# Masked keys of a dilated attention kept in residue order, and the products of its sample attention on VectorE

## The chip, the cores and the metric

The kernel runs on one core of a Trainium2 chip. The metric is the device time of one execution in microseconds (us); less is better. Engines: TensorE (PE in the rows; PEld is its weight load), VectorE (DVE), ScalarE (ACT), GpSimd (POOL) and SyncE (SP, which only issues DMAs).

## The reference

One inference step of a two-layer decoder: an attention layer, then a state-space layer, each with a squared-ReLU MLP and layer norms. There are 512 new prompt tokens and 8 sample tokens, one for each of 8 sequences with cached state. The change touches the attention layer. Its 16 heads of 64 run in three groups with dilations 1, 4 and 16:

```python
ATTN_GROUPS = ((128, 1), (512, 4), (2048, 16))
...
    scores = jnp.einsum('brnqhe,brnkhe->brnhqk', qb, kx) * SCALE
...
    scores = jnp.where(mask[None, None, :, None], scores, -jnp.inf)
    mx = jnp.max(scores, -1, keepdims=True)
    p = jnp.exp(scores - mx)
```

A prompt query of group 1 sees only keys whose position differs from its own by a multiple of 4 (group 2: of 16). A sample token attends to cached keys and values (every first, fourth or sixteenth cached position) and its own:

```python
    scores = jnp.einsum('bthe,btshe->bths', q.astype(F32), kg) * SCALE
    ...
    o = jnp.einsum('bths,btshe->bthe', p, vg) / den[..., None]
```

## The kernel before

Activations lie with features on the 128 partitions and tokens along them: 512 prompt tokens and then 8 sample tokens, 520 columns. Dense products split weights and activations into a high and a low part (`whi`, `wlo`) of a reduced fp32 type and add three products of each; they go in two halves of 260 columns (line 246). ScalarE makes the high part of weights and VectorE the low part (lines 185, 189, 196).

The order of all engines' work is written by hand. A *slot* is one dense product of 24 matmuls of 260 columns, followed by its evacuation from PSUM. Between slots, *lanes* (generators that advance by a step twice a slot) and *timers* (`self.after(n, ...)`, due n slots later) add the rest of the work. Every engine executes its own instructions in the order in which they were recorded. The attention layer walks over 8 pairs of heads (`c`) and in each over three groups (`g`): four slots for queries and keys with the rotary embedding (lines 571 to 583 on VectorE), two for values. PSUM has three banks `D` for the slots, three banks `S` for scores, transposes and the like, and two banks `V` for outputs.

What the change touches:

- `heads` (line 596), two slots after the keys: ScalarE writes `Kz`, two copies of the keys `K`, each with one head of the pair masked to zero, in the order of the tokens.
- `attn_scores` (from line 675): queries `F1` are the stationary operand, `Kz` with both heads is the moving one (line 774). Group 0 takes blocks of 128 neighbouring queries and up to 256 neighbouring keys a head. Groups 1 and 2 take residues: for residue j queries j, j+4, ... and the keys likewise, 128 a head; two residues share a bank, so that they make two blocks of scores in each group.
- `prod` (line 735): for the sample tokens, GpSimd multiplies the cached keys `ck` with the queries that a DMA has spread over the partitions (`qb`, issued two slots earlier); one slot later VectorE sums over the features (`total`, line 741).
- `attn_sample` (from line 887, in lane C): after a softmax over 16 rows, VectorE copies the weights into `sp` (lines 914, 915). GpSimd then multiplies three tiles of cached values with them and adds them up (lines 926, 930), 128 or 67 partitions by 1024 columns each; 16 small products on TensorE end the sum (line 936).

Around these, `attn_apply` scales the probabilities (VectorE, line 839, and ScalarE, line 837), transposes them on TensorE into an `S` bank (line 860), evacuates them (`pT`, lines 253 and 255) and multiplies with the values (line 853). `Kt` (lines 714, 716) is VectorE's copy of the transposed keys out of an `S` bank. After the last head pair, the outputs `o` are split into `opart` (lines 233, 234) for the output projection.

Of the kernel before, what the change touches and what calls it, by code (L numbers as in the profile page):

```python
# [11 lines left out]
AF = mybir.ActivationFunctionType  # L12
ALU = mybir.AluOpType
# [4 lines left out]
P = 128  # L18
D = 1024
KD = D // P  # L20
SEQ = 512
# [5 lines left out]
E = 64  # L27
# [52 lines left out]
class Net:  # L80
# [476 lines left out]
    def project_qk(self, g, x, cur, sqk):  # L557

        nc = self.nc
        F1, F2 = self.pair("F")  # L560
        if g != 1:
            cur["K2"] = list(self.pair("K"))
        K = cur["K2"].pop(0)
        cur["F1"][g], cur["F2"][g] = F1, K
        m = {}

        def rope_a(half):
            def f(p1):
                c0 = half * HALF
                m[half] = self.unit("ropem").rearrange("p (i t) -> p i t", i=4)  # L570
                nc.vector.tensor_tensor(out=m[half][:, 0:2], in0=p1.unsqueeze(1).broadcast_to((P, 2, HALF)),  # L571
                                        in1=self.cossin[:, :, c0:c0 + HALF], op=ALU.mult)
            return f

        def rope_b(half):
            def f(p2):
                c0 = half * HALF
                cs = slice(c0, c0 + HALF)
                t = m[half]
                nc.vector.tensor_tensor(out=t[:, 2:4], in0=p2.unsqueeze(1).broadcast_to((P, 2, HALF)),  # L580
                                        in1=self.cossin[:, :, cs], op=ALU.mult)
                nc.vector.tensor_tensor(out=F1[:, cs], in0=t[:, 0], in1=t[:, 3], op=ALU.subtract)
                nc.vector.tensor_tensor(out=F2[:, cs], in0=t[:, 2], in1=t[:, 1], op=ALU.add)
                if half:
                    self.after(1, gather)
                    self.after(2, heads)
            return f

        def gather():
            lo, hi = slice(0, 64), slice(64, P)  # L590
            nc.scalar.activation(out=K[lo], in_=F1[hi], func=AF.Copy)
            nc.scalar.activation(out=K[hi], in_=F2[hi], func=AF.Copy)
            nc.scalar.activation(out=F1[hi], in_=F2[lo], func=AF.Copy)

        def heads():
            kz = self.unit("Kz")[:, 0:2 * SEQ].rearrange("p (h t) -> p h t", h=2)
            for h in range(2):
                nc.scalar.activation(out=kz[:, h], in_=K[:, 0:SEQ], func=AF.Copy, scale=self.hmask[:, h:h + 1])
            cur["Kz"][g] = kz

        for half in range(2):
            self.slot(lambda: self.dense(self.weights(sqk, 0), x, half), rope_a(half))
            self.slot(lambda: self.dense(self.weights(sqk, 1), x, half), rope_b(half))
# [74 lines left out]
    def attn_scores(self, c, g, cur, o, late):  # L678

        nc = self.nc  # L680
        F1, F2 = cur["F1"][g], cur["F2"][g]
        kb = self.blocks(F2, g)
        out = self.O[2 + g][0, 0].rearrange("t k (c h) e -> t k c (h e)", h=2)[:, :, c, :]
# [40 lines left out]
        nk = self.NK[g]  # L724
# [9 lines left out]

        def prod():
            q = cur["qb"]
            nc.gpsimd.tensor_tensor(out=q[0:nk], in0=q[0:nk], in1=cur["ck"][g][0:nk], op=ALU.mult)  # L737
            cur["qp", g] = q

        def total():  # L740
# [2 lines left out]
        self.after(1, store)  # L743
        self.after(3, spread)
        self.after(5, prod)
        self.after(6, total)
        if g == 2:
# [7 lines left out]
        kz = cur["Kz"][g]  # L755
        both = lambda t: t.rearrange("p (h k) -> p h k", h=2)
        pts = []
        for js in ((0,), (1,), (2,), (3,)) if g == 0 else ((0, 1), (2, 3)):
            if not pts:
                pts = list(self.pair("prob"))  # L760
            pt = pts.pop(0)
            b = self.bank("S", "s", NSB)
            tiles, q0 = [], 0
            for j in js:
                if g == 0:
                    n = P if j == 0 else 2 * P
                    k0 = max(j - 1, 0) * P
                    q, ks = F1[:, j * P:(j + 1) * P], slice(k0, k0 + n)
                    mask = self.m0[:, 2 * P - n:2 * P]
                else:  # L770
                    n = P
                    q, ks = F1[:, j:SEQ:4], slice(j, SEQ, 4)
                    mask = self.m0[:, P:2 * P] if g == 1 else self.m2
                nc.tensor.matmul(both(b[:, q0:q0 + 2 * n]), q, kz[:, :, ks], start=True, stop=True)  # L774
                for h in range(2):
                    cs = slice(q0, q0 + n)
                    tiles.append((b[:, cs], pt[:, cs], mask, st[:, 1 if g else 0, j, h, g], neg[:, h, j:j + 1]))
                    for i in range(n // P):
                        key = j if g else j - (n // P - 1) + i
                        cur["P"][g, h, j, key] = pt[:, q0 + i * P:q0 + (i + 1) * P]  # L780
                    q0 += n
            a, j1 = 1 if g else 0, js[-1] + 1
            mx, ng = st[:, a, js[0]:j1, :, g, 0], neg[:, :, js[0]:j1].rearrange("p h j -> p j h")
            yield
            for sc, pr, mask, one, _ in tiles:
                nc.vector.tensor_tensor_reduce(out=pr, in0=sc, in1=mask, scale=1.0, scalar=NEG,  # L786
                                               op0=ALU.add, op1=ALU.max, accum_out=one[:, 0:1])
            nc.vector.tensor_scalar(out=ng, in0=mx, scalar1=-SCALE, scalar2=None, op0=ALU.mult)  # L788
            self.after(1, lambda tiles=tiles: self.exps(tiles))
            yield  # L790
# [96 lines left out]
    def attn_sample(self, c, cur, o):  # L887
        nc = self.nc
        nk = self.NK
# [23 lines left out]
        sp = self.sp.tile([P, 3, 16], F32, name="sp", tag="sp")  # L913
# [4 lines left out]
        v0 = cur["cv"][0]  # L918
# [4 lines left out]
        for i in range(3):  # L923
            n = nk[i]
            v = cur["cv"][i][0:n].rearrange("p b (h e) -> p (b h) e", h=2)
            nc.gpsimd.tensor_tensor(out=v, in0=v, in1=sp[0:n, i, :].unsqueeze(2).broadcast_to((n, 16, E)), op=ALU.mult)
            yield
            yield
            if i:
                nc.gpsimd.tensor_tensor(out=v0[0:n], in0=v0[0:n], in1=cur["cv"][i][0:n], op=ALU.add)  # L930
                yield
                yield
        yield
# [685 lines left out]
```

## Time and profile before

| | |
|---|---|
| median of three runs | 2050.95 us (2046.38 to 2053.96) |
| profiled execution, its own time | 2047.91 us |
| its span, first to last instruction | 2045.7 us |
| TensorE busy | 1946.1 us |
| VectorE busy | 1306.1 us |
| ScalarE busy | 938.4 us |
| GpSimd busy | 395.8 us |
| mean granted TensorE clock | 0.975 of full |

The attention layer's head pairs take the first 620 us or so of the span, its end runs to about 740 us, and the rest belongs to the MLPs and the state-space layer. Busy times are sums over instructions; the ends of matmuls are modelled, so that a row's duration is longer than the spacing of starts. How fast TensorE goes is read from the starts of successive rows in its timeline.

### The profile page before, as it was taken

How to read it: one execution, taken by the hardware profiler on the slowest of the kernel's cores; microseconds unless marked ns; L12 is line 12 of the kernel's file. 1: busy time of each engine (PE TensorE's matmuls, PEld its weight loads, DVE VectorE, ACT ScalarE, POOL GpSimd, SP SyncE). 2: the span in 40 equal slices, each digit the busy share in tenths (PEclk: the TensorE clock that was granted, in tenths of full speed). 3: DMA queues.
4: the chain of work that ended last, by engine and by line, in shares of the span. 5: the costliest groups of instructions: out<-in, count | busy, mean ns of one | idle time of the engine just before them, and what ended most of it. 6: DMA issues, size and time to landing. Idle time of an engine off the chain costs nothing. (4 is left out here: it accounts for less than half of the span.)

```text
span 2045.7 us, 38476 instructions
## 1 busy us (share of the span) xinstructions
PE 1946.1 (95%) x15530; PEld 1863.7 (91%) x15530; DVE 1306.1 (64%) x2597; ACT 938.4 (46%) x2071; POOL 395.8 (19%) x230
## 2 busy tenths in 40 slices
PE   7999999999999899999999998988999898999997
PEld 7989898898897789999999998988999898999997
DVE  4575675766868774333335779998887875554335
ACT  4555454554545354435253554644454363425241
POOL 0030330312305330000003023322232331110002
PEclk9999999999998999999999998999999999999998
DMA  7565554455557528454653255545565759996311
GB/s 196 164 174 139 159 141 138 137 159 166 164 166 215 152 68 278 165 194 146 206 196 124 94 170 176 191 154 162 183 205 184 254 154 278 286 283 182 95 42 43
DMA packets 423194, 346.92 MB, mean 170 GB/s; under 512 B 33036, under 2 KB 408292, under 8 KB 421344
## 3 DMA queue, kind: packets, MB, share of 16 engines
q1 hardware_dynamic: 405608, 344.26, 54.4%
q10 hardware_dynamic: 17408, 0.20, 0.5%
q8 instruction: 122, 2.00, 0.4%
q14 instruction: 56, 0.46, 0.1%
HBM read 322.41 MB, written 130.99 MB: 222 GB/s over the span
## 5 line engine op out<-in xcount | busy, mean ns | idle before, releaser
L246 PE MATMUL psd<-x,whi 128*128 128x260 f32 x5920 | 1117.8, 290 | 13.1 <-DVE zz L1169 5.0
L246 PEld LDWEIGHTS psd<-x,whi 128*128 128x128 f32 x5920 | 927.2, 191 | 40.1 <-issue 23.2
L246 PE MATMUL psd<-x,wlo 128*128 128x260 f32 x2960 | 842.8, 285 | 0.5 <-DVE wlo L196 0.5
L246 PEld LDWEIGHTS psd<-x,wlo 128*128 128x128 f32 x2960 | 563.9, 191 | 0.8 <-DVE wlo L196 0.8
L196 DVE TENSOR_TENSOR wlo<-wraw,whi 128x1024 fp32r<-128x1024 f32 (+1 forms) x321 | 395.1, 1250 | 52.0 <-ACT whi L189 40.0
L246 PE MATMUL psd<-hid,whi 128*128 128x260 f32 (+2 forms) x2048 | 372.9, 284 | 7.2 <-DVE acc L484 7.2
L189 ACT ACTIVATE whi<-wraw 128x1024 fp32r<-128x1024 f32 x225 | 234.4, 1050 | 223.8 <-PE psd L246 156.4
L246 PEld LDWEIGHTS psd<-hid,whi 128*128 128x128 f32 x2048 | 318.6, 190 | 7.5 <-DVE acc L484 7.4
L246 PE MATMUL psd<-hid,wlo 128*128 128x260 f32 (+2 forms) x1024 | 290.7, 284 | 0.0
L246 PEld LDWEIGHTS psd<-hid,wlo 128*128 128x128 f32 x1024 | 194.3, 190 | 0.0
L486 DVE TENSOR_TENSOR acc<-acc,psd 128x260 f32<-128x260 f32 (+2 forms) x176 | 74.0, 423 | 168.1 <-PE psd L246 167.9
L537 DVE TENSOR_TENSOR hid<-relu,hid 128x260 fp32r<-128x260 f32 x128 | 60.7, 475 | 165.0 <-ACT hid L534 164.9
L737 POOL TENSOR_TENSOR qb<-qb,cache 128x1024 f32<-128x1024 f32 (+1 forms) x24 | 59.3, 2470 | 474.1 <-DMA qb<-newscr 351.6
L530 ACT ACTIVATE relu<-psd 128x260 f32<-128x260 f32 x128 | 49.6, 387 | 169.5 <-PE psd L246 166.5
L246 PE MATMUL psd<-ypart,whi 128*128 128x260 f32 x512 | 103.0, 299 | 13.9 <-DVE ypart L1438 4.8
L796 ACT ACTIVATE prob<-prob,neg 128x128 f32<-128x128 f32 (+1 forms) x192 | 79.7, 418 | 57.6 <-DVE neg L788 51.7
L246 PEld LDWEIGHTS psd<-ypart,whi 128*128 128x128 f32 x512 | 83.0, 198 | 16.4 <-DVE ypart L1438 5.7
L774 PE MATMUL s<-Kz,F 128*128 128x256 f32 (+1 forms) x192 | 96.1, 617 | 0.0
L571 DVE TENSOR_TENSOR ropem<-psd,trig 128x520 f32<-128x520 f32 x48 | 33.5, 698 | 92.9 <-PE psd L246 87.8
L1079 DVE SCALAR_TENSOR_TENSOR conv<-raw,cvcols,conv 128x511 f32<-128x511 f32 (+2 forms) x96 | 83.1, 865 | 7.4 <-ACT conv L1074 5.1
L489 POOL TENSOR_TENSOR ln_tot<-acc 128x260 f32<-128x260 f32 x6 | 7.1, 1188 | 361.1 <-DVE acc L486 339.1
L786 DVE CUSTOM_DVE_ANT_0 prob<-s,cb 128x128 f32<-128x128 f32 (+1 forms) x192 | 51.5, 317 | 39.8 <-PE s L774 39.2
(253 smaller groups left out, 2546.1 us busy)
## 6 DMA issues: line engine op xcount, KB each, us to landing
wraw<-in_mlp_w_dram SPq DMA_DIRECT2D x128, 512.0 KB
wraw<-in_attn_w_in_dram SPq DMA_DIRECT2D x72, 512.0 KB
wraw<-in_ssm_w_in_dram SPq DMA_DIRECT2D x49, 512.0 KB
cache<-in_cache_kv_w_dram SPq DMA_DIRECT2D x32, 512.0 KB
state<-in_state_ssm_dram SPq DMA_DIRECT2D x32, 512.0 KB
out_dram<-in_cache_kv_w_dram SPq DMA_DIRECT2D x16, 1016.0 KB
qb<-newscr SPq DMA_DIRECT2D x16, 512.0 KB
ab<-acs SPq DMA_DIRECT2D x16, 512.0 KB
```

The lines of the kernel that those rows point to most:

```text
L189: nc.scalar.activation(out=hi, in_=s.raw[0], func=AF.Copy)
L196: self.nc.vector.tensor_tensor(out=lo, in0=src, in1=hi.bitcast(F32), op=ALU.subtract)
L246: self.nc.tensor.matmul(out, a, b[:, cs], start=n == 0, stop=n == 3 * len(w) - 1)
L486: nc.vector.tensor_tensor(out=a, in0=a, in1=ps, op=ALU.add)
L530: nc.scalar.activation(out=t[:, 0], in_=ps, func=AF.Relu)
L537: nc.vector.tensor_tensor(out=h[m][1][:, cs], in0=t[:, 1], in1=h[m][0][:, cs].bitcast(F32), op=ALU.subtract)
L571: nc.vector.tensor_tensor(out=m[half][:, 0:2], in0=p1.unsqueeze(1).broadcast_to((P, 2, HALF)), in1=self.cossin[:, :, c0:c0 + HALF], op=ALU ...
L737: nc.gpsimd.tensor_tensor(out=q[0:nk], in0=q[0:nk], in1=cur["ck"][g][0:nk], op=ALU.mult)
L774: nc.tensor.matmul(both(b[:, q0:q0 + 2 * n]), q, kz[:, :, ks], start=True, stop=True)
L786: nc.vector.tensor_tensor_reduce(out=pr, in0=sc, in1=mask, scale=1.0, scalar=NEG, op0=ALU.add, op1=ALU.max, accum_out=one[:, 0:1])
L796: self.nc.scalar.activation(out=pr, in_=pr, func=AF.Exp, scale=SCALE, bias=ng, accum_out=st[:, 1:2])
L1079: nc.vector.scalar_tensor_tensor(out=t[:, j:SEQ], in0=raw[:, 0:SEQ - j], scalar=w[:, 3 - j:4 - j], in1=t[:, j:SEQ], op0=ALU.mult, op1=ALU.add)
```

## The change

`Kz` of groups 1 and 2 is written in the order of residues: all keys at positions 0, 4, 8, ..., then 1, 5, 9, ..., and so on. ScalarE reads `K` in steps of 4 columns and writes neighbouring ones; the score products of these groups then read 128 neighbouring columns of each head. The queries, still the stationary operand, are taken in steps of 4 as before. Besides, the products `prod` and the products and sums over the cached values are issued on VectorE and no longer on GpSimd: 24 + 24 + 16 instructions.

```diff
@@ heads, line 596
+            src = K[:, 0:SEQ] if g == 0 else K[:, 0:SEQ].rearrange("p (m r) -> p r m", r=4)
             for h in range(2):
-                nc.scalar.activation(out=kz[:, h], in_=K[:, 0:SEQ], func=AF.Copy, scale=self.hmask[:, h:h + 1])
+                dst = kz[:, h] if g == 0 else kz[:, h].rearrange("p (r m) -> p r m", r=4)
+                nc.scalar.activation(out=dst, in_=src, func=AF.Copy, scale=self.hmask[:, h:h + 1])
@@ prod, line 737
-            nc.gpsimd.tensor_tensor(out=q[0:nk], in0=q[0:nk], in1=cur["ck"][g][0:nk], op=ALU.mult)
+            nc.vector.tensor_tensor(out=q[0:nk], in0=q[0:nk], in1=cur["ck"][g][0:nk], op=ALU.mult)
@@ attn_scores, line 772
-                    q, ks = F1[:, j:SEQ:4], slice(j, SEQ, 4)
+                    q, ks = F1[:, j:SEQ:4], slice(j * P, (j + 1) * P)
@@ attn_sample, lines 926 and 930
-            nc.gpsimd.tensor_tensor(out=v, in0=v, in1=sp[0:n, i, :].unsqueeze(2).broadcast_to((n, 16, E)), op=ALU.mult)
+            nc.vector.tensor_tensor(out=v, in0=v, in1=sp[0:n, i, :].unsqueeze(2).broadcast_to((n, 16, E)), op=ALU.mult)
...
-                nc.gpsimd.tensor_tensor(out=v0[0:n], in0=v0[0:n], in1=cur["cv"][i][0:n], op=ALU.add)
+                nc.vector.tensor_tensor(out=v0[0:n], in0=v0[0:n], in1=cur["cv"][i][0:n], op=ALU.add)
```

Lines after 598 stand two lines further down in the changed kernel. On TensorE, ScalarE and SyncE the same instructions stand in the same order as before.

On VectorE, here is the stretch in the second head pair in which the weights `sp` of the first pair's sample tokens come out, before the change (`wlo` is the split of projection weights, `ropem` and `F` the rotary embedding, `ss` the sum of the sample scores):

```order
L571 TENSOR_TENSOR ropem<-psd,trig 128x520
L914 COPY sp<-sP 128x32
L915 COPY sp<-sP 67x16
L255 COPY pT<-pT 128x512
L196 TENSOR_TENSOR wlo<-wraw,whi 128x8x64 x4
L580 TENSOR_TENSOR ropem<-psd,trig 128x520
L582 TENSOR_TENSOR F<-ropem 128x260
L583 TENSOR_TENSOR F<-ropem 128x260
L741 TENSOR_REDUCE ss<-qb 128x16
L839 TENSOR_SCALAR prob<-prob,fac 128x128 x4
L571 TENSOR_TENSOR ropem<-psd,trig 128x520
L716 COPY Kt<-kT 128x512
```

The same stretch on VectorE after the change:

```order
L571 TENSOR_TENSOR ropem<-psd,trig 128x520
L739 TENSOR_TENSOR qb<-qb,cache 128x1024
L916 COPY sp<-sP 128x32
...
L583 TENSOR_TENSOR F<-ropem 128x260
L743 TENSOR_REDUCE ss<-qb 128x16
L928 TENSOR_TENSOR cache<-cache,sp 128x1024
L841 TENSOR_SCALAR prob<-prob,fac 128x128 x4
L571 TENSOR_TENSOR ropem<-psd,trig 128x520
L928 TENSOR_TENSOR cache<-cache,sp 128x1024
L718 COPY Kt<-kT 128x512
```

A query product (line 739) now stands after the first rope product, and two of the value products (line 928) ahead of the copy `Kt`; the remaining three instructions of this chain follow behind it, one slot apart.

GpSimd's queue before the change, from its first product to the second head pair's:

```order
L737 TENSOR_TENSOR qb<-qb,cache 128x1024 x2
L737 TENSOR_TENSOR qb<-qb,cache 67x1024
L737 TENSOR_TENSOR qb<-qb,cache 128x1024
L926 TENSOR_TENSOR cache<-cache,sp 128x1024 x2
L930 TENSOR_TENSOR cache<-cache 128x1024
```

After it, GpSimd's first work is that of the layer's end:

```order
L426 TENSOR_TENSOR acc<-x 128x520 x8
L489 TENSOR_TENSOR ln_tot<-acc 128x260
L491 TENSOR_TENSOR ln_tot<-ln_tot,acc 128x260 x6
```

All its instructions between the head pairs' start and there are gone.

## Rows read from the trace of the kernel before

**Rows 1.** The page, part 1: engine, busy us (share of span), instructions.

```profile
PE 1946.1 (95%) x15530; PEld 1863.7 (91%) x15530; DVE 1306.1 (64%) x2597; ACT 938.4 (46%) x2071; POOL 395.8 (19%) x230
```

**Rows 2.** Waits of TensorE, 0 to 620 us: us in total, times, longest.

```profile
PE pT L860 <- DVE Kt L716: 9.6, 5, 2.0
```

**Rows 3.** Timeline of TensorE, group 0: start us, us, engine, line, operation, tiles, count.

```profile
56.23 0.28 PE L246 MATMUL psd<-x,wlo 128*128 128x260 f32 x1
56.35 1.02 PE L774 MATMUL s<-Kz,F 128*128 128x512 f32 x2
56.81 0.80 PE L246 MATMUL psd<-x,whi 128*128 128x260 f32 x2
57.44 0.28 PE L246 MATMUL psd<-x,wlo 128*128 128x260 f32 x1
```

**Rows 4.** Timeline of TensorE, a block of scores of group 2.

```profile
98.21 2.08 PE L774 MATMUL s<-Kz,F 128*128 128x256 f32 x4
99.70 0.82 PE L246 MATMUL psd<-x,whi 128*128 128x260 f32 x2
100.36 0.28 PE L246 MATMUL psd<-x,wlo 128*128 128x260 f32 x1
```

**Rows 5.** Timeline of GpSimd, 131 to 145 us.

```profile
131.91 4.22 POOL L926 TENSOR_TENSOR cache<-cache,sp 128x1024 f32<-128x1024 f32 x2 [2.57 <-issue]
...
141.33 2.74 POOL L930 TENSOR_TENSOR cache<-cache 67x1024 f32<-67x1024 f32 x1
```

**Rows 6.** Timeline of VectorE, 130 to 148 us; in brackets the idle time before.

```profile
130.98 0.70 DVE L571 TENSOR_TENSOR ropem<-psd,trig 128x520 f32<-128x520 f32 x1 [1.04 <-PE psd L246]
...
132.45 9.35 DVE L196 TENSOR_TENSOR wlo<-wraw,whi 128x512 fp32r<-128x512 f32 x4
...
142.44 1.92 DVE L582 TENSOR_TENSOR F<-ropem 128x260 f32<-128x260 f32 x1
144.29 0.42 DVE L583 TENSOR_TENSOR F<-ropem 128x260 f32<-128x260 f32 x1
...
147.14 0.68 DVE L716 COPY Kt<-kT 128x512 f32<-128x512 f32 x1
```

**Rows 7.** Timeline of TensorE, the first of the five waits.

```profile
147.87 0.55 PE L860 MATMUL pT<-cb,prob 128*128 128x128 f32 x3 [1.98 <-DVE Kt L716]
```

**Rows 8.** Line 774 by itself: weight loads, ns least/median/most, first and last start.

```profile
L774 PEld LDWEIGHTS s<-Kz,F x192: 187/310/333, 49.2 to 655.7; 128*128 128x128 f32 x192
```

**Rows 9.** Timeline of TensorE, transposes of keys in steps of 4.

```profile
70.13 0.65 PE L694 MATMUL kT<-cb,K 128*128 128x128 f32 x4
70.61 0.27 PE L700 MATMUL nT<-cb,F 128*8 128x128 f32 x1
```

**Rows 10.** Line 1467, another layer's sum of two SBUF tiles on VectorE.

```profile
L1467 DVE TENSOR_TENSOR state<-state,Bb x8: 1217/1219/1222, 1672.8 to 1859.4; 128x1024 f32<-128x1024 f32 x8
```

**Rows 11.** Windows: length, busy us of each engine, granted clock (PEclk), DMA share, GB/s.

```profile
226.00:233.00 7.00, 5.17 (x32) 4.68 (x33) 5.40 (x22) 3.59 (x9) 0.00 (x0) 0.76 0.70 206
...
640.00:660.00 20.00, 17.47 (x97) 14.00 (x98) 13.53 (x33) 8.12 (x23) 7.37 (x3) 0.74 0.81 249
```

**Rows 12.** Timelines of VectorE and TensorE, 638 to 644 us.

```profile
638.87 4.23 DVE L234 TENSOR_TENSOR opart<-o,opart 128x520 fp32r<-128x520 f32 x2 [0.26 <-ACT opart L233]
...
640.38 0.39 PE L246 MATMUL psd<-opart,whi 128*128 128x260 f32 x1 [1.10 <-DVE opart L234]
...
643.15 0.58 PE L246 MATMUL psd<-opart,whi 128*128 128x260 f32 x1 [2.15 <-DVE opart L234]
```

**Rows 13.** Timelines of ScalarE and TensorE, masked keys and their scores, group 2.

```profile
79.15 1.32 ACT L598 ACTIVATE Kz<-K,cb 128x512 f32<-128x512 f32 x2
...
93.39 2.08 PE L774 MATMUL s<-Kz,F 128*128 128x256 f32 x4
```

**Rows 14.** Timelines of GpSimd and VectorE, a query product and VectorE's place for it.

```profile
207.71 2.40 POOL L737 TENSOR_TENSOR qb<-qb,cache 128x1024 f32<-128x1024 f32 x1 [26.94 <-PE s L774]
...
211.01 0.70 DVE L571 TENSOR_TENSOR ropem<-psd,trig 128x520 f32<-128x520 f32 x1 [0.29 <-PE psd L246]
```

## The prediction

> **What bounds the kernel now.** I read the busy times first: TensorE is busy 1946 of 2046 us, VectorE 64% [rows 1]. So time is won where TensorE itself works slowly or where it waits. The waits of TensorE in the first 620 us (the attention layer) come second: one kind stands out, five waits of about 1.9 us, 9.6 us together, of a transpose of the probabilities for VectorE's copy of the transposed keys [rows 2]. Everything else there runs without a gap, so a microsecond taken out of TensorE's own instructions in this stage is a microsecond of the span.
>
> Third, the timeline of TensorE around two kinds of score products. Products of fp32 operands show as two records each. In the first group two records read 512 neighbouring columns each; from their start to the start of the weight product behind the next pair 56.35 to 57.44, 1.09 us pass [rows 3]. In the other groups four records read 256 columns each, every fourth of `Kz`: the same 1024 columns, with the same pair behind them, take 98.21 to 100.36, 2.15 us [rows 4]. Ordinary weight products start 0.12 us apart [rows 3], so the pair is 0.24 us of both; 256 neighbouring columns cost (1.09 - 0.24) / 4 = 0.21 us, 256 strided ones (2.15 - 0.24) / 4 = 0.48 us.
>
> Fourth, what makes VectorE late at the five waits: GpSimd's chain of products and sums over the cached values runs from 131.91 to 144.07 [rows 5]; in that stretch VectorE's four weight splits take 9.35 us and a subtraction of 260 columns 1.92 us, while the like one right after GpSimd has ended takes 0.42 [rows 6]. VectorE's instructions with two operands in SBUF thus stand still while GpSimd has one of its own. `Kt` is copied at 147.14, and TensorE, waiting since 145.89, goes on at 147.87 [rows 6, 7].
>
> **The sum.** It is made against the profiled execution, 2047.91 us with a span of 2045.7; the median of the three runs is 2050.95, 3 us above it, inside their own spread of 7.6.
>
> (a) *Scores from neighbouring columns.* Groups 1 and 2 have two blocks of four records in each of 8 head pairs: 32 blocks, each 2.15 - 1.09 = 1.06 us dearer than neighbouring columns, 33.9 us in all. The stationary operand `F1[:, j:SEQ:4]` stays strided: its load takes 310 ns at the median against 187 at the least [rows 8]. The first load of a block has only a 0.12 us product to hide under, so I charge it the difference, 0.12 us. The later three lie under 0.21 us products. If all of a 310 ns load had to pass, each would add 0.10, 0.42 a block in all. But the transposes of the keys also load strided fp32 weights and start (70.61 - 70.13) / 4 = 0.12 us apart, as ordinary products do [rows 9], so a load's latency is longer than the time that it holds the array up. I take 1.06 - 0.12 = 0.94 us a block: **30.1 us**, with ends 20.5 (0.64 a block) and 33.9.
>
> (b) *The five waits.* One instruction of 128x1024 with two SBUF operands costs VectorE 1219 ns when undisturbed [rows 10], 0.61 us per 512 columns. In the chain above VectorE lost 9.35 - 4 x 0.61 = 6.9 and 1.92 - 0.42 = 1.5, 8.4 us. In the new order three moved instructions stand ahead of that `Kt` copy, 3 x 1.22 = 3.7 us. So `Kt` is ready some 4.7 us sooner, at about 143.1 instead of 147.8. TensorE asks at 145.9, or 1 us sooner by (a): 1.8 us to spare, and the waits go: **9.6 us**.
>
> (c) *The clock after them.* [...]
>
> (d) *The end of the layer.* At 640 and 643 TensorE waits 1.10 and 2.15 us for the splits of `opart`, whose two instructions take 4.23 us [rows 12], as long as the splits of (b) did beside GpSimd; at 0.70 each, as the rope product of 520 columns takes [rows 6], they save 2.8. The 20 us from 640 on have a granted clock of 0.74 [rows 11], a loss of 5.2; I count half, 2.5, since later idle stretches there stay: **5.3 us**, ends 0 and 8.
>
> (e) *What VectorE takes over.* 24 products of queries and keys, 24 of values and weights, 16 sums: 64 x 1.22 = 78 us. Before, GpSimd's 64 cost VectorE about as much by blocking it (8.4 us for the five of one head pair, against 6.1), so its load hardly rises, and at 64% it isn't the bound. If none is exposed this costs 0, if every one delays TensorE 78 us. The nearest row is the chain in (b), which has room, so I charge **2 us**.
>
> (f) *At no cost.* ScalarE now reads `K` in steps of four when it writes `Kz`. A pair of these takes 1.32 us [rows 13]. No row shows such a read on ScalarE; bounds are 1.32 and, at TensorE's own ratio 0.48 / 0.21, 3.0 us. The tightest place of groups 1 and 2 has the pair done at 79.15 + 1.32 = 80.47 and the scores at 93.39, 12.9 us of cover [rows 13]; what queues behind it on ScalarE (exponentials, copies of `V`) is later by 1.7 us at worst, twice in a head pair, on an engine that is busy 46% [rows 1]. No DMA changes its place on SyncE's queue. A product now waits in VectorE's queue for the query rows that a DMA spreads: GpSimd started one at 207.71, so they had landed, and VectorE comes to its place after the rope product of 211.01 ends at 211.71, 4 us later [rows 14]. That is the least cover that I found in the even stretch, and the block taken out of it by (a) leaves 3 us.
>
> Sum: 30.1 + 9.6 + 5.0 + 5.3 - 2 = 48; 2047.9 - 48 = **2000 us**.
>
> **The rivals.**
>
> *The loads pace the scores.* If a strided load can't lie under the product before it, the records go on following at about 0.48 us though their columns are neighbours: (a) falls to nothing, and the change would not do what it says for the scores. 2048 - 20 + 2 = 2030 us. Against it: key transposes at 0.12 us with loads of that kind [rows 9], and neighbouring 512-column records whose loads cost nothing visible [rows 3]. Chance 5%. [...]
>
> *The products take GpSimd's place.* VectorE works strictly in order, and two products stand right before the `Kt` copy. If the probabilities' transposes still find their bank occupied, (b) to (d) are lost: 2048 - 30 = 2018 us at the most. The 1.8 us to spare speak against it. Chance 10%; half of it lost would be 2008.
>
> *Slower: VectorE held by the spread of the queries.* All 24 query products now stand in VectorE's queue before weight splits and rope products. Should the spread land later than VectorE arrives, TensorE runs out of split weights. From 3 us beyond today's landing on, each microsecond costs 24; the gain of 48 is used up at 2 us more, 5 us late; 7 us late would be 2000 + 24 x 4 = 2096 us. Speaking for it: before, only GpSimd waited there, with nothing urgent behind. Against: 4 us of cover [rows 14]; and the landing follows TensorE's slots as VectorE's place does, so both come earlier together. Chance 2%.
>
> **How the numbers follow.** Forecast 83%, rivals 5, 10 and 2%. The bounds of (a) and (d) alone give 2000 + 10 + 5 = 2015 and 2000 - 4 - 3 - 2 = 1991. With the second rival and the 3 us between profile and median, the range is 1988 to 2018. About 0.5%, 10 us, is what a measurement of this kernel can tell from no change. Only loads that pace the scores together with half-kept waits come within it (2%); slower is the third rival (2%); faster 96%.
>
> **What would show it.** In the profile after: score records of groups 1 and 2 some 0.21 to 0.24 us apart, a block with its pair near 1.2 us; the row of TensorE waiting for `Kt` gone from the waits; weight splits in the attention layer at 0.7 us throughout; GpSimd idle there; the 64 products on VectorE near 1.22 us. I am wrong in (a) if the block stays above 1.5 us, in (b) and (e) if TensorE's waits for VectorE in the first 620 us sum to over 5 us, in (f) if VectorE waits for the spread or TensorE for `Kz`.

## The result, and the profile after

| | before | after |
|---|---|---|
| median of four runs | 2049.73 us | 1999.84 us (1998.01 to 2001.34) |
| ratio, 95% interval | | 0.9763 (0.9743 to 0.9783) |
| profiled execution: its own time, span | 2047.91, 2045.7 us | 1999.22, 1997.2 us |
| mean granted TensorE clock | 0.975 | 0.978 |

The kernel became 2.4% faster, some 49 us, and the forecast of 2000 us held. Part 1 of the page of the changed kernel (engine, busy us, share, instructions), beside [rows 1]:

```profile
PE 1909.8 (96%) x15530; PEld 1851.4 (93%) x15530; DVE 1287.1 (64%) x2661; ACT 953.7 (48%) x2071; POOL 244.9 (12%) x166
```

VectorE has 64 instructions more, 78 us of work, and is busy 19 us less. Its other instructions thus take about 97 us less than beside GpSimd's products, an estimate from these two busy times. ScalarE has the same instructions and is busy 15 us longer.

The waits of TensorE, 0 to 620 us, in the changed kernel (us in total, times, longest), beside [rows 2]:

```profile
PE xT L312 <- DMA xtok<-in_x_prompt_dram: 5.0, 1, 5.0
PE vT L662 <- ACT Vt L667: 3.4, 1, 3.4
...
PE sT L897 <- DVE ss L743: 1.4, 1, 1.4
...
PE pT L862 <- ACT Vt L667: 0.7, 1, 0.7
```

The row of `Kt` is gone. What is left lies in the first 40 us of the program (`xT` and three smaller rows, as before), in one place of 0.7 us as before, and in the end of the layer, which now begins at 596 us and so falls into this stretch (`vT`, `sT`, a wait of 1.1 us for `opart`).

TensorE's timeline at a block of scores of group 2 in the changed kernel (start us, us, engine, line, tiles), beside [rows 4]:

```profile
94.74 1.19 PE L776 MATMUL s<-Kz,F 128*128 128x256 f32 x4
95.58 0.59 PE L246 MATMUL psd<-x,whi 128*128 128x260 f32 x2
96.01 0.28 PE L246 MATMUL psd<-x,wlo 128*128 128x260 f32 x1
```

From 94.74 to 96.01 the block with its pair takes 1.27 us; the same block took 2.15. Over all 32 blocks the median is 1.27 (1.24 to 1.38), and before 2.15 (2.10 to 2.36), leaving out the five that held a `Kt` wait as well; unrounded, 2.152 - 1.266 = 0.89 us less.

VectorE's timeline in the changed kernel, the stretch of [rows 6] one head pair's chain long (in brackets the idle time before):

```profile
126.56 0.70 DVE L571 TENSOR_TENSOR ropem<-psd,trig 128x520 f32<-128x520 f32 x1 [1.74 <-PE psd L246]
127.17 1.22 DVE L739 TENSOR_TENSOR qb<-qb,cache 128x1024 f32<-128x1024 f32 x1
...
129.09 2.48 DVE L196 TENSOR_TENSOR wlo<-wraw,whi 128x512 fp32r<-128x512 f32 x4
...
132.21 0.43 DVE L582 TENSOR_TENSOR F<-ropem 128x260 f32<-128x260 f32 x1
...
134.03 1.22 DVE L928 TENSOR_TENSOR cache<-cache,sp 128x1024 f32<-128x1024 f32 x1
...
136.56 1.22 DVE L928 TENSOR_TENSOR cache<-cache,sp 128x1024 f32<-128x1024 f32 x1
137.69 0.69 DVE L718 COPY Kt<-kT 128x512 f32<-128x512 f32 x1
```

The four splits take 2.48 us where they took 9.35, and the subtraction of 260 columns 0.43 where it took 1.92. From the first rope product to `Kt` 11.13 us pass; before it was 147.14 - 130.98 = 16.16 [rows 6]. `Kt` is copied by 138.38, and TensorE comes to the transposes of the probabilities behind it 2.0 us later, without a wait:

```profile
140.42 0.60 PE L862 MATMUL pT<-cb,prob 128*128 128x128 f32 x4
```

VectorE runs undisturbed like this up to 577 us. In the last head pair GpSimd's sums of the layer's end (line 426, 577.66 to 597.41) stand beside VectorE, and there one split takes 1.94 us where the like ones take 1.21, and one product of cached values 2.33 where the others take 1.22.

The clock over the even part of the layer, one window each (us, busy us of PE, PEld, DVE, ACT, POOL, granted clock, DMA share, GB/s), first of the kernel before, then of the changed one:

```profile
40.00:600.00 560.00, 549.73 (x4159) 497.70 (x4158) 378.10 (x926) 286.91 (x777) 121.86 (x51) 0.99 0.54 152
```

```profile
40.00:600.00 560.00, 558.20 (x4463) 522.44 (x4462) 400.83 (x1062) 329.27 (x851) 14.28 (x8) 1.00 0.59 169
```

The end of the layer did not become even. TensorE's timeline there in the changed kernel, from the first product of the output projection, beside the last two of [rows 12]:

```profile
596.52 0.39 PE L246 MATMUL psd<-opart,whi 128*128 128x260 f32 x1
598.02 0.39 PE L246 MATMUL psd<-opart,whi 128*128 128x260 f32 x1 [1.11 <-DVE opart L234]
...
615.55 0.23 PE L897 MATMUL sT<-cb,ss 67*16 67x67 f32 x1 [1.41 <-DVE ss L743]
619.15 1.13 PE L662 MATMUL vT<-cb,V 128*128 128x128 f32 x4 [3.37 <-ACT Vt L667]
...
626.65 0.99 PE L862 MATMUL pT<-cb,prob 128*128 128x128 f32 x4 [3.56 <-ACT Vt L667]
...
672.56 0.60 PE L359 MATMUL ln<-ln_tot,ones_d 128*128 128x260 f32 x2
```

The same two points in the kernel before:

```profile
638.89 0.39 PE L246 MATMUL psd<-opart,whi 128*128 128x260 f32 x1
...
719.79 0.60 PE L359 MATMUL ln<-ln_tot,ones_d 128*128 128x260 f32 x2
```

They divide the gain. The first product of the output projection starts at 596.52 instead of 638.89: 42.4 us. The first sum of the layer norm behind it starts at 672.56 instead of 719.79: 47.2. The span is 48.5 shorter. The 1.3 us behind the norm I don't explain. That part has the same instructions in all kernels here, and from the first product with the MLP's `hid` to the last transposition of the outputs it took between 1235 and 1243 us in the profiled executions, 1235 and 1241 in the two of the changed kernel.

### The profile page after: what moved, and what is told of

It reads as the page before. It is cut to its first block, busy times and chain, and to the rows that moved or that the text cites. A ratio compares the mean times of both kernels' runs of the same rounds, so it can differ in the third digit from the quotient of the medians.

```text
span 1997.2 us, 38379 instructions
## 1 busy us (share of the span) xinstructions
PE 1909.8 (96%) x15530; PEld 1851.4 (93%) x15530; DVE 1287.1 (64%) x2661; ACT 953.7 (48%) x2071; POOL 244.9 (12%) x166
## 5 line engine op out<-in xcount | busy, mean ns | idle before, releaser
L196 DVE TENSOR_TENSOR wlo<-wraw,whi 128x1024 fp32r<-128x1024 f32 (+1 forms) x321 | 348.7, 1105 | 54.4 <-ACT whi L189 42.2
L426 POOL TENSOR_TENSOR acc<-x 128x520 f32<-128x520 f32 x8 | 14.3, 1805 | 582.7 <-PE nT L702 577.2
L246 PE MATMUL psd<-ypart,wlo 128*128 128x260 f32 x256 | 74.9, 293 | 0.0
L776 PE MATMUL s<-Kz,F 128*128 128x256 f32 (+1 forms) x192 | 67.9, 462 | 0.0
L1157 ACT ACTIVATE raw<-psd 128x260 f32<-128x260 f32 x64 | 24.4, 382 | 89.9 <-PE psd L246 89.7
```

What stands on the lines that cost most here:

```text
L196: self.nc.vector.tensor_tensor(out=lo, in0=src, in1=hi.bitcast(F32), op=ALU.subtract)
L246: self.nc.tensor.matmul(out, a, b[:, cs], start=n == 0, stop=n == 3 * len(w) - 1)
L426: nc.gpsimd.tensor_tensor(out=acc[m], in0=x[m][0].bitcast(F32), in1=x[m][1].bitcast(F32), op=ALU.add)
L1157: nc.scalar.activation(out=raws[i][:, cs], in_=ps, func=AF.Copy)
```

## The experiments

### One half of the change at a time

The keys alone: three lines go back to GpSimd.

```diff
-            nc.vector.tensor_tensor(out=q[0:nk], in0=q[0:nk], in1=cur["ck"][g][0:nk], op=ALU.mult)
+            nc.gpsimd.tensor_tensor(out=q[0:nk], in0=q[0:nk], in1=cur["ck"][g][0:nk], op=ALU.mult)
...
-                nc.vector.tensor_tensor(out=v0[0:n], in0=v0[0:n], in1=cur["cv"][i][0:n], op=ALU.add)
+                nc.gpsimd.tensor_tensor(out=v0[0:n], in0=v0[0:n], in1=cur["cv"][i][0:n], op=ALU.add)
```

> Only the keys in residue order; all 64 products stay on GpSimd. Theory: the two parts of the change are separate terms. In the changed kernel a block of scores with its pair of products takes 1.27 us at the median instead of 2.16, 32 x 0.89 = 28.5 us. The five waits for Kt stay, and since Kt does not move while TensorE comes 0.9 us sooner, each gets 0.9 us longer: 28.5 - 4.5 = 24 us less, 2026 us, five waits of about 2.8 us, and ScalarE's masked keys at 1.2 us as in the changed kernel. Rival (the keys do nearly all of it): 2000 to 2010 us, waits gone.

The products alone: lines 597 to 600 and 774 as before the change, the products on VectorE.

> Only the 64 products moved to VectorE; the scores read every fourth column as before. Theory: the five waits (9.6 us), three half-clock windows (5 us) and about 4 us at the end of the layer go: 18 us less, 2032 us; score blocks stay at 2.16 us. Rival (keys do nearly all): 2045 us or more. Rival (products take GpSimd's place): the waits for Kt stay, 2045 to 2055 us.

Measured: the keys alone 2033.2 us, ratio 0.9922 (0.9908 to 0.9937), some 16 us; the products alone 2025.16 us, 0.9884 (0.9869 to 0.9899), some 24 us. Both ratios gain 40 us together, the whole change 49, so some 9 us belong to neither half. The traces show it more sharply: TensorE starts the output projection 12.0 us sooner with the keys alone (626.85), 15.9 sooner with the products alone (623.03) and 42.4 sooner with both, so that 14.5 us there need both halves. The keys alone fell short of their expectation, and the products alone, expected at 2032 us, did better than theirs. The wait for `Kt` with the keys alone, TensorE, 0 to 620 us:

```profile
PE pT L862 <- DVE Kt L718: 14.0, 5, 2.9
```

And the 10 us around the first of the five, as a window (granted clock third from the end), of the same kernel; the other four read 0.83 as well:

```profile
140.00:150.00 10.00, 7.20 (x44) 6.67 (x44) 6.65 (x27) 5.56 (x11) 1.53 (x1) 0.83 0.39 105
```

The keys' gain of 32 x 0.89 = 28.5 us is there, block by block. But TensorE comes to the five places sooner, while `Kt` still comes when GpSimd lets VectorE go: the waits are 14.0 us instead of 9.6. The clock falls after all five, where before it fell after three (0.83 in such windows there, 1.00 after the first and the fifth): 2 x 0.17 x 10 = 3.4 us more. So 7.8 us of the 28.5 are handed back there. Just ahead of the output projection this kernel's timeline of TensorE has two further waits:

```profile
622.71 0.48 PE L862 MATMUL pT<-cb,prob 128*128 128x128 f32 x1 [4.15 <-DVE prob L841]
625.01 0.69 PE L862 MATMUL pT<-cb,prob 128*128 128x128 f32 x2 [1.82 <-DVE prob L841]
```

Both are for the scaling of probabilities on VectorE, four instructions that take 10.53 us while GpSimd runs its products and sums without a pause; in the kernel before, the median of one is 0.28 us. VectorE's timeline:

```profile
614.62 10.53 DVE L841 TENSOR_SCALAR prob<-prob,fac 128x128 f32<-128x128 f32 x4
```

The granted clock from 615 us to the output projection is 0.79, another 2.5 us. Up to there 30 of the 32 blocks lie, and 26.7 - 7.8 - 6.0 - 2.5 = 10.4 us, against the 12.0 measured: the shortfall is accounted for to within 2 us. With the products alone the mean clock of 40 to 620 us is 1.00, and the row of `Kt` is gone.

### Which products matter

The 40 instructions over the cached values on VectorE, all else as before the change:

> Of the products only the 40 over the cached values go to VectorE; the 24 query products stay on GpSimd, scores as before. Theory: the value chain of 12 us without a pause is what holds VectorE up ahead of Kt, so nearly all of the gain of the moved products is here: waits for Kt gone, 14 to 17 us less, 2033 to 2036 us. Rival (it is the number of GpSimd's instructions that counts, 40 of 64): about 11 us less, 2038.

The 24 query products on VectorE, all else as before the change:

> Of the products only the 24 query products go to VectorE; the value chain stays on GpSimd, scores as before. Theory: the five waits for Kt stay, a little longer by the product that now stands ahead of them; 0 to 3 us less, 2047 to 2050 us. Rival (number of instructions, 24 of 64): 7 us less, 2043.

Measured: the values alone 2027.53 us, 0.9896 (0.9878 to 0.9914), faster than I expected and close to all products together; the row of `Kt` is gone there too. The queries alone 2056.55 us, 1.0042 (1.0031 to 1.0053): slower by some 9 us, where I expected a small gain. TensorE's wait in that kernel, 0 to 620 us:

```profile
PE pT L860 <- DVE Kt L716: 15.4, 5, 3.1
```

VectorE's timeline there, the chain of [rows 6]:

```profile
131.09 0.70 DVE L571 TENSOR_TENSOR ropem<-psd,trig 128x520 f32<-128x520 f32 x1 [1.74 <-PE psd L246]
131.71 1.22 DVE L737 TENSOR_TENSOR qb<-qb,cache 128x1024 f32<-128x1024 f32 x1
...
133.62 9.41 DVE L196 TENSOR_TENSOR wlo<-wraw,whi 128x512 fp32r<-128x512 f32 x4
...
148.35 0.67 DVE L716 COPY Kt<-kT 128x512 f32<-128x512 f32 x1
```

The query product stands ahead of `sp`, which starts GpSimd's chain. The whole chain, with the time that VectorE loses to it, moves back by 1.2 us: from the rope product to `Kt` 17.26 us instead of 16.16. Nothing is taken off GpSimd in that stretch to pay for it. The waits grew by 5.8 us, and in the 10 us around them the clock's loss sums to 10.9 instead of 5.1; the output projection starts 12.6 us later. So one product of 1.22 us ahead of a chain that stays on GpSimd costs more than its own length, and the same product beside the moved chain costs nothing that the times show (2025.16 us with the query products moved too, 2027.53 without).

### What the stationary operand in steps of four costs

A probe: the score products take 128 neighbouring columns of the queries, so that each block holds the scores of other queries.

```diff
-                    q, ks = F1[:, j:SEQ:4], slice(j * P, (j + 1) * P)
+                    q, ks = F1[:, j * P:(j + 1) * P], slice(j * P, (j + 1) * P)
```

> The changed kernel, but groups 1 and 2 take 128 neighbouring queries as the stationary operand where every fourth is due: other queries' scores, the same work. Theory: the rest of the block's cost over neighbouring columns (1.27 against 1.09 us with its pair) is the strided load of the queries: loads fall from 320 to 190 ns, blocks to 1.09 to 1.12 us, 32 x 0.16 = 5 us less than the changed kernel's 2000, 1995 us. Rival (the four-record block has a cost of its own, or two heads' columns do): blocks stay near 1.27 us, 2000 us.

Measured in a single run: 1993.75 us. A single time does not tell 5 us (a single run of the kernel with strided writes, below, took 1995.57 us, and its output projection starts when that of the changed kernel does), so the trace has to: the output projection starts at 592.3 us instead of 596.5. The weight loads of this line (ns least/median/most), first of the changed kernel, then of the probe:

```profile
L776 PEld LDWEIGHTS s<-Kz,F x192: 187/320/332, 48.4 to 606.5; 128*128 128x128 f32 x192
```

```profile
L776 PEld LDWEIGHTS s<-Kz,F x192: 186/189/193, 48.9 to 602.5; 128*128 128x128 f32 x192
```

A block with its pair takes 1.10 us at the median (1.08 to 1.20), as neighbouring columns in group 0 do [rows 3]. The strided load thus costs 1.266 - 1.101 = 0.16 us a block and 5.3 us in all. The load itself is 0.13 us longer.

### The moved products: room and landing

The query products one slot sooner, nearer to the landing of their spread:

```diff
-        self.after(5, prod)
-        self.after(6, total)
+        self.after(4, prod)
+        self.after(5, total)
```

> The changed kernel with the query products and the sums over them one slot sooner, one slot after the spread was issued and no longer two. It tests the rival in which VectorE waits for the spread's landing. Theory: the cover was 3 us, a slot is 2.9 us: VectorE waits 0 to 1 us for some of the 24, in sum under 12 us, TensorE rides over it on its banks: 2000 to 2004 us. Rival (landing is on VectorE's path): 2 us or more each, 24 x 2 = 48 us, 2040 us and more.

Measured 2000.56 us, 0.9752 (0.9724 to 0.978), like the changed kernel. Idle time of VectorE ahead of line 739 (us, times), first in the changed kernel, then one slot sooner:

```profile
  DMA qb<-newscr: 0.3, 1
```

```profile
  DMA qb<-newscr: 5.9, 4
```

With a slot less of cover the landing does show, in 4 of 24 places. Three of them (1.66, 1.05 and 1.09 us, before 200 us) leave no wait on TensorE. The fourth, at the layer's end, does: VectorE's and then TensorE's timeline,

```profile
617.11 1.22 DVE L739 TENSOR_TENSOR qb<-qb,cache 67x1024 f32<-67x1024 f32 x1 [2.15 <-DMA qb<-newscr]
```

```profile
618.73 0.58 PE L246 MATMUL psd<-opart,whi 128*128 128x260 f32 x1 [2.72 <-DVE acc L484]
```

The sum `acc` stands right behind that product in VectorE's queue. So VectorE's slack swallows the landing in the even stretch and not at the layer's end.

Each query product and each sum of the values with a second instruction beside it whose result nothing reads: 40 instructions, 49 us.

```diff
+            ck = cur["ck"][g][0:nk]
+            nc.vector.tensor_tensor(out=ck, in0=ck, in1=ck, op=ALU.mult)
...
+                nc.vector.tensor_tensor(out=cur["cv"][i][0:n], in0=cur["cv"][i][0:n], in1=cur["cv"][i][0:n], op=ALU.mult)
```

> The changed kernel with 40 more VectorE instructions of the same kind (1.22 us each, on tiles that are dead then): one behind each query product and one behind each sum of the values, 49 us of VectorE work. It tests whether VectorE's added work lies off TensorE's path. Theory: there is room; of 49 us less than 8 come through, 2000 to 2008 us, no wait of TensorE for Kt over 0.5 us before 590 us. Rival (VectorE's room is used up): 25 to 49 us more, 2025 to 2049, with waits for Kt back.

Measured 2008.82 us, 0.9793 (0.9769 to 0.9818): 6 us (by the ratios) to 9 us (by the medians) of the 49 come through, about the 8 that I had set as the limit. TensorE's waits of that kernel that differ from the changed kernel's, 0 to 620 us:

```profile
PE pT L864 <- ACT Vt L667: 4.1, 6, 0.7
...
PE kT L696 <- DVE sp L919: 1.2, 1, 1.2
```

No wait for `Kt` has come back. What is late first is ScalarE's `Vt`, by 0.7 us at six places, one in a head pair (one place in the changed kernel), and then the layer's end. The single load of moved work is therefore near the edge of the room, not beyond it. For `Kt` the test is a mild one: of the 40 only one stands ahead of it in the stretch of [rows 6], where it is copied 139.46 - 127.07 = 12.39 us after the rope product instead of 11.13, and TensorE comes 1.7 us after it instead of 2.0.

### Where the stride should stand

ScalarE reads neighbouring keys and writes them 128 columns apart:

```diff
-            src = K[:, 0:SEQ] if g == 0 else K[:, 0:SEQ].rearrange("p (m r) -> p r m", r=4)
+            src = K[:, 0:SEQ] if g == 0 else K[:, 0:SEQ].rearrange("p (m r) -> p m r", r=4)
...
-                dst = kz[:, h] if g == 0 else kz[:, h].rearrange("p (r m) -> p r m", r=4)
+                dst = kz[:, h] if g == 0 else kz[:, h].rearrange("p (r m) -> p m r", r=4)
```

> The changed kernel with ScalarE reading neighbouring keys and writing them 128 columns apart (same result, the stride on the other side). The changed kernel's masked keys took up to 1.295 us against 0.71 before. Theory: it is the reading in steps of 16 bytes that costs, writing apart costs nothing: 0.71 us each, ScalarE 15 us less busy, the span unchanged (2000 us within 0.3%), since the pair has over 10 us of cover. Rival (any step costs ScalarE): 1.2 us or more each, span unchanged as well.

VectorE puts queries and keys of groups 1 and 2 into residue order as it makes them, so that ScalarE, the key transposes and both operands of the scores read neighbours:

```diff
+            out = F[:, 0:SEQ].rearrange("p (r m) -> p m r", r=4)[:, m0:m0 + n // 4]
+            nc.vector.tensor_tensor(out=out, in0=v(a), in1=v(b), op=op)
...
-                    q, ks = F1[:, j:SEQ:4], slice(j * P, (j + 1) * P)
+                    q, ks = F1[:, j * P:(j + 1) * P], slice(j * P, (j + 1) * P)
```

> A version built on the changed kernel: VectorE writes queries and keys of groups 1 and 2 in the order of residues right at the rotary embedding, so that the masking, the transposes of the keys and both operands of the scores use neighbouring columns. Theory: score blocks with their pair fall from 1.27 to 1.09 us (5 us in all), the transposes of keys lose 0.01 us each (0.8 us), ScalarE's masked keys return to 0.71 us: 5 to 6 us less than the changed kernel, 1994 us, if VectorE's writes 128 columns apart cost nothing (0.43 us for 260 columns). Rival: such writes cost VectorE 1.5 times or more; then still 1994 to 2000, with VectorE busier by 64 x 0.2 = 13 us.

The changed kernel again, timed beside it:

> The changed kernel itself, on the same chip as the version before it. Theory: 2000 us, ratio to the kernel before 0.976.

Measured: 1995.57 us in a single run for the first, 1991.27 us, 0.9726 (0.9704 to 0.9748), for the second, and 1997.28 us, 0.9752 (0.9731 to 0.9773), for the changed kernel on the same chip. Durations of the instructions that make `Kz` (ns least/median/most): in the changed kernel 707/1207/1295, with strided writes

```profile
L600 ACT ACTIVATE Kz<-K,cb x48: 708/1198/1257, 38.2 to 578.5; 128x512 f32<-128x512 f32 x48
```

and with VectorE's residue order, where the strided writes are VectorE's (428/430/433 for 260 columns in the changed kernel)

```profile
L612 ACT ACTIVATE Kz<-K,cb x48: 707/713/722, 37.9 to 572.8; 128x512 f32<-128x512 f32 x48
L583 DVE TENSOR_TENSOR F<-ropem x64: 599/628/656, 45.9 to 567.4; 128x260 f32<-128x260 f32 x32, 128x252 f32<-128x252 f32 x32
```

On ScalarE reading every fourth column and writing 128 columns apart cost the same, 0.5 us; that writing apart would be free is refuted. On VectorE, which reads neighbours here and writes 128 columns apart, it costs 0.2 us an instruction, and VectorE's busy time on the page grows from 1287.1 to 1296.9 us: ten microseconds of an engine with room. The score blocks fall to 1.10 us (1.08 to 1.20), and the output projection starts at 590.7 instead of 596.5 and, in the second run of the changed kernel, 598.0. Its median is 6 us below that of the changed kernel; the two intervals still overlap a little, so that the traces carry this more than the times.

### The wait that stayed at the layer's end

After the change GpSimd's last work beside the head pairs, eight sums of the inputs (line 426), still runs beside the first split of `opart`, which takes 1.46 us there and 0.69 elsewhere. Those sums on VectorE, in the changed kernel and in the one with VectorE's residue order:

```diff
-            nc.gpsimd.tensor_tensor(out=acc[m], in0=x[m][0].bitcast(F32), in1=x[m][1].bitcast(F32), op=ALU.add)
+            nc.vector.tensor_tensor(out=acc[m], in0=x[m][0].bitcast(F32), in1=x[m][1].bitcast(F32), op=ALU.add)
```

> The changed kernel, with the eight sums of the input's two parts (line 426, the last work that GpSimd has in the attention layer, 128x520, 1.3 to 2.3 us each there) on VectorE instead. Theory: the wait of 1.1 us for opart that stayed at the start of the output projection (the split of opart takes 1.46 us beside such a sum, 0.70 otherwise) goes, as it did where only the products were moved and the sums fell elsewhere; eight sums of about 0.70 us find room on VectorE. 1 us directly and up to 2 by the clock behind it: 1995 to 2000 us beside 1997 to 2000 for the changed kernel; no instruction of VectorE in the attention layer above its undisturbed time. Rival: in the last head pair VectorE is short of room already, and 5.6 us more of work delays a split or a rope product: another wait of 1 to 6 us takes its place, 2000 to 2006 us.

> The kernel in which VectorE writes queries and keys in residue order as it makes them, with the same eight sums on VectorE. Theory: two waits for opart stand there (0.92 and 1.09 us); both go, 2 to 5 us: 1986 to 1990 us beside the 1991 of that kernel. Rival: VectorE, which has 19 us more of work there already, becomes late in the last head pair: 1991 to 1997 us.

Measured: 1998.32 us, 0.9756 (0.973 to 0.9782), and 1992.33 us, 0.973 (0.9704 to 0.9756). Neither differs from its kernel without the move, so that the gain expected of the second, 1986 to 1990 us, did not come. TensorE's waits from 560 to 740 us, first in the changed kernel, then with the sums moved:

```profile
PE pT L862 <- ACT Vt L667: 3.6, 1, 3.6
...
PE vT L662 <- ACT Vt L667: 3.4, 1, 3.4
...
PE psd L246 <- DVE opart L234: 1.4, 2, 1.1
...
PE psd L246 <- DVE acc L484: 0.3, 1, 0.3
```

```profile
PE pT L862 <- ACT Vt L667: 4.3, 1, 4.3
...
PE vT L662 <- ACT Vt L667: 3.0, 1, 3.0
...
PE psd L246 <- DVE acc L484: 1.2, 2, 0.7
...
PE psd L246 <- DVE opart L234: 0.6, 2, 0.3
```

Most of the wait of 1.1 us for `opart` goes, as the theory says (0.35 us of it stay), and the waits behind it do not shrink with it: those for `acc` and for the second `Vt` are longer, that for the first is shorter. Such single waits differ by as much between two executions of the changed kernel (3.6 and 4.1 us for the second `Vt`, 3.4 and 2.7 for the first), so they alone show little. What holds is the time of the first `Vt` copy: it starts at 618.50 us in the changed kernel and at 618.56 with the sums moved. ScalarE's queue shows what this `Vt` waits for, in the changed kernel (ACTq is its sequencer, which issues the DMAs):

```profile
609.95 0.65 ACTq L806 DMA_DIRECT2D st<-st  x1
...
617.82 0.64 ACTq L807 DMA_DIRECT2D st<-st  x1
618.50 0.60 ACT L667 ACTIVATE Vt<-vT 128x512 f32<-128x512 f32 x1 [7.07 <-DMA st<-st]
```

Eight small transfers of softmax statistics, 0.64 us each to issue, stand in ScalarE's queue ahead of this copy, the first that TensorE waits for there, and take 8.5 us from the first to the end of the last, with gaps between them; before the change it was 6.7. The copy starts right behind them. With the sums moved the copy again starts 0.05 us after the last of the eight is issued. So what TensorE saves ahead of this point is waited for before or at it. That these transfers set its time is read from the two queues; no run takes them away, and why there are gaps I have not tried.

## Why the prediction was right, step by step

| step | predicted | measured |
|---|---|---|
| (a) scores | 30.1 | 32 x 0.89 = 28.5 |
| (b) waits for `Kt` | 9.6 | 9.6, the row is gone |
| (c) clock after them | 5.0 | 3 x 1.7 = 5.1, an estimate from the clock |
| (d) end of the layer | 5.3 | about 3, of it 0.2 in waits |
| (e) VectorE's new work | -2 | 0 before the layer's end |
| (f) other edits | 0 | 0 |

Up to the output projection 30 of the 32 blocks lie: 26.7 + 9.6 + 5.1 = 41.4 us of the 42.4 measured there. From there to the layer norm 80.9 us became 76.0; less the two blocks there, 1.8 us, some 3 remain for (d).

(a) was right in its mechanism and a little too large. The records do follow at nearly the pace of neighbouring columns (1.27 us a block with its pair against 1.10 in the probe), and the strided load is what is left. I charged 0.12 us a block for it, the difference of two durations of the load; the probe with neighbouring queries measures 0.16. The rival by which loads pace the scores would have kept the block at about 2.15 us and is refuted by 1.27. That all four loads of a block pass, 0.42 us, is refuted by the probe too.

(b) came as worked out. I said that `Kt` would come 4.7 us sooner; in the rows it came 16.16 - 11.13 = 5.0 sooner. The splits take 0.62 us each where I counted 0.61.

No run shows the 5.0 us that (c) has in the sum as a time of its own; what the traces show is the granted clock. In the kernel before it is 0.76 in the 7 us around the second wait [rows 11], and the same around the third and the fourth (third from the end):

```profile
307.00:314.00 7.00, 5.09 (x30) 4.29 (x29) 5.95 (x24) 3.04 (x7) 0.00 (x0) 0.76 0.79 230
389.00:396.00 7.00, 5.13 (x32) 4.80 (x33) 5.44 (x23) 3.55 (x8) 0.00 (x0) 0.76 0.70 215
```

Inside the stretch around the second wait, in each microsecond from 229 to 232, it is 0.50. In the 10 us around each of the three waits it is 0.83, and 3 x 0.17 x 10 = 5.1 us is an estimate from that. The clock followed the waits: with them gone the granted clock of 40 to 600 us is 1.00 in the changed kernel, and where they stayed and grew to between 2.8 and 3.1 us (the keys alone, the query products alone) it fell at all five places.

The runs agree with my reading that GpSimd's chain holds up VectorE's splits: four of them take 2.48 us with the chain moved, 9.35 with the keys alone and 9.41 with the query products alone. Not every instruction of VectorE is held up: in the kernel before, while GpSimd's sum of 141.33 runs [rows 5], a rope product that reads `psd` out of PSUM takes 0.69 us, and the subtraction behind it, with both operands in SBUF, 1.92 [rows 6]:

```profile
141.72 0.69 DVE L580 TENSOR_TENSOR ropem<-psd,trig 128x520 f32<-128x520 f32 x1
```

(d) is the term that was mis-sized. I let both waits for `opart` go; the second, 2.15 us, went, and the first, 1.1 us, stayed, because it stood beside GpSimd's sums of line 426, which the change does not move. The step that failed goes further, though: I counted a wait at its full length where another queue was due soon after. The waits for `Vt` grew from 2.1 and 2.6 us to 3.4 and 3.6, a wait of 1.41 for `ss` came up, and in the run with the sums moved the first wait for `opart` was worth nothing that the time shows either. From the first product of the output projection to the layer norm all of TensorE's waits sum to 10.5 us before and 10.3 after, so of the 2.8 us that I charged for the two waits 0.2 came. What (d) did bring is mostly the clock, of which I had counted 2.5: over these two stretches the granted clock is 0.89 and 0.91 (third from the end), a loss of 8.9 and of 6.8 us.

```profile
638.89:719.79 80.90, 70.05 (x499) 60.78 (x498) 58.24 (x116) 27.65 (x65) 27.30 (x16) 0.89 0.61 181
```

```profile
596.52:672.56 76.04, 65.62 (x499) 58.86 (x498) 56.28 (x124) 27.52 (x65) 7.89 (x8) 0.91 0.65 193
```

(e) was charged 2 us and cost nothing before the layer's end. 49 us more of such work cost 6 to 9 us, so the room is not large, and the first to give way is `Vt`. The rival in which the products take GpSimd's place at `Kt` is refuted by the row that is gone: 2.0 us are to spare there, where I had worked out 1.8. A load of 1.2 us more ahead of `Kt` did not bring the wait back either; a larger one was not tried. That rival's price was wrong, though: where the waits for `Kt` stay, (a) is not kept whole, and the nearest run, the keys alone, came to 2033 us and not to the 2018 that I gave. That the order of steps matters was not in my text: of the moved products one group alone loses 9 us, since it comes ahead of GpSimd's chain without shortening it.

(f) held. A pair of `Kz` takes 2.34 us at 77.65 us in the changed kernel, between my bounds of 1.32 and 3.0, and TensorE never waits for it. VectorE waited for the spread of the queries once, 0.3 us; by my own sign that is a miss, but a wait of this size is far from the slower rival. The cover was smaller than the 3 us that I had read from one place: a slot sooner, some 2.9 us (24 products 0.12 us apart), VectorE waited 1.05 to 1.66 us at three places of the even stretch, which leaves about 1.2 to 1.9 us there, and at the layer's end 2.15 us, with a wait of TensorE behind it.

Two more signs held only up to the last head pair: GpSimd idle, and splits undisturbed throughout. The eight sums of line 426 run there from 577.66 us on.

What I did not foresee is that the terms are not independent. I added (a) to (b), as if either could be had alone. The keys alone keep some 16 of their 28.5 us, because time saved ahead of a copy that comes no sooner lengthens the wait for it.

That the sum met the time to within 1 us is partly luck. (a) and (d) were too large by about 4 us together; (e)'s 2 us were not spent, and 2.3 us, 1.0 ahead of the output projection and 1.3 behind the norm, stand in no term.

## What to carry to other kernels

A gain on the engine that bounds the kernel counts only as far as the next thing it waits for comes sooner too (the keys alone kept some 16 of their 28.5 us); look for that wait first, and take its cause away in the same change. Moving work off GpSimd paid here by what it had held up on VectorE (four splits 9.35 us beside its chain, 2.48 without), so move whole chains: a part of the chain that stays can be pushed later by the part that was moved (`Kt` by 1.2 us with the query products alone). Taking fp32 columns that are not neighbours had a price on each of the three engines that did it here, 1.5 to 2.3 times the time, so let an engine with room pay it, once, as early as the data is made.

## What the runs showed of the hardware

I had not expected the stride to cost ScalarE this much, and as much for writing as for reading: 512 fp32 elements a partition read in steps of 16 bytes take 1.21 us, and written in steps of 512 bytes (128 columns) 1.20, against 0.71. VectorE pays less, 0.63 against 0.43 us for some 256 elements a partition written in steps of 512 bytes; it was not timed with a step of 16. TensorE's moving operand, in steps of 16 bytes, paid 0.48 against 0.21 us for 256 columns [rows 3, 4], and its strided load 0.32 against 0.19, of which a block of four saw 0.16 in all.

So in fp32 a step of four elements, or of 128, took from 1.5 times (VectorE) over 1.7 (ScalarE, and TensorE's load) to 2.3 times (TensorE's moving operand) as long as neighbours. What sets these prices no run shows.
